# Low parts of eight weight units made by accumulating transfers instead of subtractions, in the last stages of a one-layer hybrid decoder

## The chip, the cores and the metric

The kernel runs on one core of one Trainium2 chip. The metric is the device time of one execution in microseconds (us); of several runs the median is given. The core has five engines with a queue each, worked off in order: TensorE (PE) multiplies, VectorE (DVE) and ScalarE (ACT) work elementwise, GpSimd (POOL) and SyncE (SP) here mostly issue transfers (DMAs), which run on 16 DMA engines.

## The reference, cut to what matters

One layer is computed for 512 prompt tokens and 64 sample tokens, 576 together. All arrays are fp32. The part around the change is the end of the layer:

```
h2 = rms_norm(x, g_ffn)
x = x + (silu(h2 @ w_ffn_gate) * (h2 @ w_ffn_up)) @ w_ffn_down      # 1024 -> 2816 -> 1024
h3 = rms_norm(x, g_ple)
gate = sigmoid(h3 @ w_ple_gate)                                      # 1024 -> 1024
emb = p @ w_ple_proj                                                 # 256 -> 1024
x = x + gate * emb
y = rms_norm(x, g_final)
```

Ahead of it stand the pooling and recurrent branches, a merge and an output projection.

## The kernel before, in words

All activations lie transposed: a tile has 128 features on the partitions and 576 tokens in the free dimension, in two halves of 288. `res[0]` to `res[7]` hold the residual x.

**Hi and lo.** A product in nearly full fp32 precision is made of three: weight and activation are each split into a high part (rounded to fp32r) and a low part (the rest), and `mm` (lines 141 to 160) accumulates hi*hi (line 153), hi*lo (line 155) and lo*hi (line 157) in PSUM, for both halves: 6 matmuls for each block of 128 input features. A weight "unit" is a tile of 128 x 1024 floats (512 KB). Each unit is loaded by SP into `raw` (line 70, two buffers) and split into `whi` and `wlo` (line 74, three buffers each).

There are two ways to split. `split_piece` (lines 76 to 79) copies `raw` to `whi` on ScalarE and subtracts `raw - whi` into `wlo` on VectorE. `split_dma` (lines 81 to 91) copies `raw` to `whi` on ScalarE, but rounds the negated copy `-raw` into `wlo`, also on ScalarE (line 87), and then POOL issues a DMA that reads the unit from HBM once more and adds it into `wlo` (line 88). With `hi_first` the copy to `whi` is line 86, ahead of the negation. `split` (lines 93 to 99) chooses by whether it was given a source `src`.

**Order of units.** `seq` (lines 102 to 113) lists the units in the order of their use. Its last part is `plain0` = 36 to 43 (gate and up units of the FFN), then from `dn0` = 44 on four down units (44 to 47, for the last four of 22 blocks of FFN features) and eight units of `w_ple_gate` (48 to 55). `next_unit` (lines 131 to 135) hands out unit i and calls `ahead` (lines 117 to 129), which issues loads up to unit i+4 and splits up to unit i+2. Line 126 says which units are split by DMA. The last two units take buffers of their own (line 125).

**The stages around the change.** The FFN runs in pairs of products by a fast matrix scheme (`pair`, lines 969 to 1029, and `drain`, lines 1049 to 1057), TensorE's order there being fixed by `in_order` (line 137) which holds up to line 1238. Then come:

- the down stage (lines 1154 to 1168): for each of eight output blocks m, 24 matmuls on the activations `ac` with half a down unit (12 first for m = 0 and for m = 1, then the other 12 of each); PSUM banks "c", "d" for even m and "a", "b" for odd m, two buffers each. Then VectorE adds the two halves to `res[m]` (line 1166), `scale_split` makes the high part `h3h` on ScalarE (line 241) and the low part `h3l` on VectorE (line 242), and `add_square` makes the square on ScalarE (lines 249, 252) and adds it to `ssum` on VectorE (line 253);
- ahead of it in the program, the embedding's inputs: two tiles of `p` are loaded, copied and split (lines 1141 to 1147, `pth`, `ptl`), and the two tiles of `w_ple_proj` are loaded into one buffer `wpe` and split (lines 1148 to 1151);
- the gate stage (lines 1217 to 1235): embedding product 0 (12 matmuls), gate products 0 and 1 (48 each), with the norm's `rms` in the middle of gate product 1, embedding product 1, and products 2 and 3; then blocks 4 to 7 in two parts by tokens (lines 1241 to 1283), and the final norm.

Within the limits that are written out (`in_order`, `issue_after`, `high_priority`), a scheduler puts each engine's instructions in order, by the program's order and by when it takes their inputs to be ready. Each queue then waits in that order.

Of the kernel before, what the change touches and what calls it, by code (L numbers as in the profile page):

```python
# [28 lines left out]
def trunk(ctx: ExitStack, tc: tile.TileContext, a, o):  # L29
# [13 lines left out]
    def pool(name, bufs=1, space=None, side=None):  # L43
        es[name] = ExitStack()
        kw = {} if space is None else {"space": space}
        if side:
            kw["side"] = side
        es_pool[name] = es[name].enter_context(tc.tile_pool(name=name, bufs=bufs, reuse_waits="tile", **kw))
        return es_pool[name]
# [18 lines left out]
    def raw_load(src, n=1024):  # L68
        raw = wp.tile([P, 1024], F32, name="raw", tag="raw", bufs=2)
        nc.sync.dma_start(out=raw[:, 0:n], in_=src)  # L70
        return raw

    def hi_lo(pl=wp, tag="", bufs=3):
        return [pl.tile([P, 1024], F32R, name="w" + n, tag="w" + n + tag, bufs=bufs) for n in ("hi", "lo")]

    def split_piece(raw, u, cs):
        hi, lo = u
        nc.scalar.copy(out=hi[:, cs], in_=raw[:, cs])  # L78
        tt(out=lo[:, cs], in0=raw[:, cs], in1=hi[:, cs].bitcast(F32), op=SUB)  # L79

    def split_dma(raw, u, src, hi_first=False):

        n = src.shape[-1]
        raw, hi, lo = (t[:, 0:n] for t in (raw, *u))
        if hi_first:
            nc.scalar.copy(out=hi, in_=raw)
        neg = act(lo, raw, AF.Copy, scale=-1.0)  # L87
        nc.gpsimd.dma_start(out=lo, in_=src, accum_op=ADD)  # L88
        if not hi_first:
            with tc.issue_after(neg.ins):  # L90
                nc.scalar.copy(out=hi, in_=raw)  # L91

    def split(raw, n=1024, src=None, **kw):
        u = hi_lo(**kw)
        if src is None:
            split_piece(raw, u, slice(0, n))
        else:
            split_dma(raw, u, src, True)
        return u
# [5 lines left out]
    up0 = len(seq)  # L105
    seq += [up[i] for i in range(KD)]
    out0 = len(seq)
    seq += [a["w_out"][m] for m in range(KD)]
    plain0 = len(seq)
    for m in range(NPL):  # L110
        seq += [a["w_ffn_gate"][m], a["w_ffn_up"][m]]
    dn0 = len(seq)
# [4 lines left out]
    def ahead(n_raw, n_split):  # L117
        while state["raw"] < min(n_raw, state["lim"]):
            i = state["raw"]
            raws[i] = raw_load(seq[i], seq[i].shape[-1])  # L120
            state["raw"] += 1
        while state["split"] < min(n_split, state["lim"]):
            i = state["split"]

            kw = dict(pl=es_pool["fp"], tag="z", bufs=2) if i >= len(seq) - 2 else {}
            if plain0 <= i < dn0 or i in (dn0 + 1, dn0 + 2) or up0 + 4 <= i < out0 and i % 2:
                kw["src"] = seq[i]
            splits[i] = split(raws.pop(i), seq[i].shape[-1], **kw)
            state["split"] += 1

    def next_unit():
        i = state["use"]
        state["use"] += 1
        ahead(i + 5, i + 3)
        return splits.pop(i)
# [57 lines left out]
    for k in range(5, KD):  # L193
        load_x(k)
    state["raw"] = state["split"] = state["use"] = 2
    ahead(3, 0)


# [95 lines left out]
    for k in range(KD):  # L294
# [7 lines left out]
        with tc.high_priority(offset=-0):  # L302
# [4 lines left out]
            else:  # L307
                sq = tmp.tile([P, T], F32, name="sq", tag="ta")
                act(sq, res[k], AF.Square)
                tt(out=ssum2, in0=ssum2, in1=sq, op=ADD)  # L310
    last_add = tt(out=ssum, in0=ssum, in1=ssum2, op=ADD)
    ahead(5, 3)
    u2 = next_unit()
    mm(zp[2], u2, hx, ks=range(0, 3))
# [45 lines left out]
    def tmpa():  # L360
        return tmp.tile([P, T], F32, name="ta", tag="ta")
# [699 lines left out]
    fp = pool("fp")  # L1061
# [76 lines left out]
    fp = pool("fp")  # L1138
    pe, wpe = [], []
    hx3 = [(fp.tile([P, T], F32R, name=f"h3h{k}"), fp.tile([P, T], F32R, name=f"h3l{k}")) for k in range(KD)]  # L1140
    for k in range(2):
        pn = tmpa()
# [5 lines left out]
    for e in range(2):  # L1148
        pn = fp.tile([P, 1024], F32, name="wpe", tag="wpe", bufs=1)
        nc.sync.dma_start(out=pn, in_=a["w_ple_proj"][e])  # L1150
        wpe.append(split(pn, pl=fp, tag="e", bufs=2))
    ssum = pers.tile([P, T], F32, name="ssum", tag="ssum")
    pzs = [two_banks() for _ in range(2)]
    u = next_unit()
# [193 lines left out]
def build(shapes):  # L1348
    import concourse.bacc as _bacc
    nc = _bacc.Bacc("TRN2", target_bir_lowering=False, num_devices=1, dynamic_dma_scratch_size=4096)  # L1350
    a = {n: nc.dram_tensor(f"in_{n}", s, F32, kind="ExternalInput").ap() for n, s in shapes.items()}
    o = {n: nc.dram_tensor(f"out_{n}", s, F32, kind="ExternalOutput").ap() for n, s in _OUTS}
    with tile.TileContext(nc, schedule_with_timeline_sim=False) as tc:
        trunk(tc, a, o)
    return nc
# [16 lines left out]
```

## Time and profile before

| | us |
|---|---|
| median of three runs | 836.67 (836.52 to 840.22) |
| the profiled execution, its time | 838.23 |
| its span, first to last instruction | 836.2 |
| TensorE busy | 822.1 (98%) |
| VectorE busy | 605.6 (72%) |
| ScalarE busy | 504.5 (60%) |
| GpSimd busy | 114.1 (14%) |

A row of the timeline gives the start in us from the span's start, the duration in us, the engine (PE, DVE, ACT, POOL, SP), the line of the kernel, the operation, the tiles as out<-in, and, in square brackets, the idle time of the engine before it and what ended it. A matmul's duration of 0.29 us overlaps the next one's. The names `bc`, `bd`, `ba`, `bb` are PSUM banks. "DMA to landing" is the time from a transfer's issue until its data has arrived, as lowest, median and highest.

### The profile page before, as it was taken

The numbers are of one execution on the slowest core, as the hardware profiler recorded it, in microseconds if no ns is written. First come the engines' busy times: TensorE is split into PE (matmuls) and PEld (weight loads), VectorE is DVE, ScalarE is ACT, GpSimd is POOL, SyncE is SP. The second block draws the span as 40 slices with busy tenths as digits, with TensorE's granted clock in tenths as the row PEclk, the third lists the DMA queues.
The fourth block names the chain that finished last, engine by engine and source line by source line (L and its number), as shares of the span: only waits on it lengthen the run. The fifth ranks groups of instructions, "written<-read, shape, count | busy, mean of one in ns | idle before, by whom it ended". The sixth has DMA issues, their size and how long they took to land.

```text
span 836.2 us, 15184 instructions
## 1 busy us (share of the span) xinstructions
PE 822.1 (98%) x6092; PEld 807.7 (97%) x6092; DVE 605.6 (72%) x1005; ACT 504.5 (60%) x826; POOL 114.1 (14%) x194
## 2 busy tenths in 40 slices
PE   8999999999999999999999999999999999999996
PEld 6999899999999999999999999999999999998996
DVE  7877776764787776547988688777787777558846
ACT  7356435666777665446667667766676666645534
POOL 6304110000111110000111121112211121000000
PEclk9999999999999999999999999999999999999998
DMA  7521220322747674246866787657777678453103
GB/s 233 164 84 51 76 105 29 126 105 80 181 107 183 165 172 140 76 108 144 186 130 142 149 208 194 157 123 175 181 173 164 132 158 214 113 156 101 52 1 113
DMA packets 38758, 111.95 MB, mean 134 GB/s; under 512 B 4896, under 2 KB 8992, under 8 KB 38688
## 3 DMA queue, kind: packets, MB, share of 16 engines
q1 hardware_dynamic: 24000, 74.51, 27.1%
q0 software_dynamic: 12528, 33.30, 23.5%
q10 hardware_dynamic: 2160, 3.19, 1.0%
q8 instruction: 47, 0.77, 0.4%
q14 instruction: 23, 0.19, 0.1%
HBM read 105.98 MB, written 5.00 MB: 133 GB/s over the span
## 4 chain that ended last, share of the span: by engine, by line
PE 91%; DVE 3%; DMA 2%; ACT 1%; issue 1%; POOL 1%; SPq 0%; DVEq 0%
PE bb L872 7%; PE bb L873 7%; PE bb L874 7%; PE mm L155 5%; PE mm L153 5%; PE mm L157 5%; PE ba L874 4%; PE ba L873 4%; PE ba L872 4%; PE bd L874 2%; PE bd L873 2%; PE bd L872 2%; PE bc L873 2%; PE bc L874 2%; PE bc L872 2%; PE ba L153 2%
## 5 line engine op out<-in xcount | busy, mean ns | idle before, releaser
L78 ACT CAST whi<-raw 128x1024 fp32r<-128x1024 f32 (+2 forms) x48 | 46.6, 972 | 70.6 <-PE mm L155 32.8
L153 PE MATMUL mm<-hh,whi 128*128 128x288 f32 x320 | 71.2, 304 | 1.1 <-DVE ta L358 0.9
L155 PE MATMUL mm<-hl,whi 128*128 128x288 f32 x320 | 70.8, 301 | 1.3 <-DVE hl L242 1.3
L157 PE MATMUL mm<-hh,wlo 128*128 128x288 f32 x320 | 69.5, 299 | 0.4 <-DVE wlo L79 0.4
L87 ACT ACTIVATE wlo<-raw 128x1024 fp32r<-128x1024 f32 (+1 forms) x49 | 49.2, 1004 | 26.3 <-PE ba L874 18.4
L79 DVE TENSOR_TENSOR wlo<-raw,whi 128x1024 fp32r<-128x1024 f32 (+2 forms) x48 | 56.7, 1184 | 10.4 <-ACT whi L78 9.8
L857 DVE TENSOR_TENSOR clo<-raw,chi 128x1024 fp32r<-128x1024 f32 (+1 forms) x38 | 43.3, 1140 | 27.8 <-ACT chi L853 27.7
L153 PEld LDWEIGHTS mm<-hh,whi 128*128 128x128 f32 x320 | 52.9, 193 | 4.0 <-ACT whi L78 1.6
L155 PEld LDWEIGHTS mm<-hl,whi 128*128 128x128 f32 x320 | 52.3, 191 | 2.5 <-DVE hl L242 1.9
L157 PEld LDWEIGHTS mm<-hh,wlo 128*128 128x128 f32 x320 | 52.3, 191 | 0.7 <-DVE wlo L79 0.6
L857 DVE TENSOR_TENSOR wlo<-rb,whi 128x1024 fp32r<-128x1024 f32 (+1 forms) x38 | 43.3, 1139 | 10.9 <-ACT whi L853 10.7
L853 ACT CAST chi<-raw 128x1024 fp32r<-128x1024 f32 (+1 forms) x38 | 36.9, 971 | 9.8 <-DVE raw L849 9.8
L853 ACT CAST whi<-rb 128x1024 fp32r<-128x1024 f32 (+1 forms) x38 | 37.3, 982 | 6.3 <-PE bb L873 2.8
L87 ACT ACTIVATE dl<-rb 128x512 fp32r<-128x512 f32 (+1 forms) x38 | 22.7, 598 | 30.0 <-PE bc L874 28.2
L1006 ACT ACTIVATE bc<-bb 128x288 f32<-128x288 f32 x38 | 15.0, 395 | 41.6 <-PE bb L874 41.6
L91 ACT CAST whi<-raw 128x1024 fp32r<-128x1024 f32 (+1 forms) x37 | 36.0, 972 | 0.0
L843 DVE TENSOR_TENSOR rb<-rb 128x512 f32<-128x512 f32 (+1 forms) x38 | 24.6, 647 | 8.0 <-ACT dh L91 8.0
L882 DVE TENSOR_TENSOR cz<-bc,p 128x288 f32<-128x288 f32 x38 | 17.3, 456 | 14.6 <-PE bc L874 14.3
L879 DVE TENSOR_TENSOR cz<-bb,p 128x288 f32<-128x288 f32 x38 | 17.3, 456 | 14.2 <-PE bb L874 9.1
L848 DVE TENSOR_TENSOR raw<-raw,rb 128x512 f32<-128x512 f32 (+1 forms) x38 | 24.6, 647 | 1.2 <-ACT whi L91 0.5
L88 POOL DMA_DIRECT2D wlo<-in_w_ffn_gate x13 | 11.1, 855 | 103.8 <-ACT wlo L87 103.8
L849 DVE TENSOR_TENSOR raw<-raw 128x512 f32<-128x512 f32 (+1 forms) x38 | 24.6, 647 | 0.8
(789 smaller groups left out, 3227.6 us busy)
## 6 DMA issues: line engine op xcount, KB each, us to landing
raw<-in_w_in SPq DMA_DIRECT2D x26, 512.0 KB, 3.4
raw<-in_w_ffn_gate SPq DMA_DIRECT2D x13, 512.0 KB, 4.1
raw<-in_w_ffn_up SPq DMA_DIRECT2D x13, 512.0 KB, 5.3
wlo<-in_w_ffn_gate POOLq DMA_DIRECT2D x13, 512.0 KB, 5.5
wlo<-in_w_ffn_up POOLq DMA_DIRECT2D x13, 512.0 KB, 6.3
rb<-in_w_ffn_gate SPq DMA_DIRECT2D x9, 512.0 KB, 4.6
rb<-in_w_ffn_up SPq DMA_DIRECT2D x9, 512.0 KB, 5.3
raw<-in_w_dn SPq DMA_DIRECT2D x12, 384.0 KB, 3.7
```

The lines of the kernel that those rows point to most:

```text
L78: nc.scalar.copy(out=hi[:, cs], in_=raw[:, cs])
L79: tt(out=lo[:, cs], in0=raw[:, cs], in1=hi[:, cs].bitcast(F32), op=SUB)
L87: neg = act(lo, raw, AF.Copy, scale=-1.0)
L91: nc.scalar.copy(out=hi, in_=raw)
L153: nc.tensor.matmul(out=out[h], lhsT=wh, rhs=xh[:, h * HT:(h + 1) * HT], start=first, stop=False)
L155: nc.tensor.matmul(out=out[h], lhsT=wh, rhs=xl[:, h * HT:(h + 1) * HT], start=False, stop=False)
L157: i = nc.tensor.matmul(out=out[h], lhsT=wl, rhs=xh[:, h * HT:(h + 1) * HT], start=False, stop=last)
L853: nc.scalar.copy(out=tiles[0][:, 0:2 * q["W"]], in_=q[raw][:, 0:2 * q["W"]])
L857: tt(out=lo, in0=q[raw][:, 0:2 * q["W"]], in1=hi.bitcast(F32), op=SUB)
L872: nc.tensor.matmul(out=out, lhsT=wh, rhs=xh, start=k == 0 and not seeded, stop=False, **kw)
L873: nc.tensor.matmul(out=out, lhsT=wh, rhs=xl, start=False, stop=False, **kw)
L874: i = nc.tensor.matmul(out=out, lhsT=wl, rhs=xh, start=False, stop=k == n - 1, **kw)
```

## The change

`split_dma` takes the place of `split_piece` for eight units: down units 44 and 47 (45 and 46 had it before), gate units 48 to 51, and the two tiles of the embedding's projection. Units 52 to 55 keep the subtraction.

```diff
@@ -123,7 +123,7 @@
             i = state["split"]
 
             kw = dict(pl=es_pool["fp"], tag="z", bufs=2) if i >= len(seq) - 2 else {}
-            if plain0 <= i < dn0 or i in (dn0 + 1, dn0 + 2) or up0 + 4 <= i < out0 and i % 2:
+            if plain0 <= i < dn0 or dn0 <= i < dn0 + 8 or up0 + 4 <= i < out0 and i % 2:
                 kw["src"] = seq[i]
             splits[i] = split(raws.pop(i), seq[i].shape[-1], **kw)
             state["split"] += 1
@@ -1148,7 +1148,7 @@
     for e in range(2):
         pn = fp.tile([P, 1024], F32, name="wpe", tag="wpe", bufs=1)
         nc.sync.dma_start(out=pn, in_=a["w_ple_proj"][e])
-        wpe.append(split(pn, pl=fp, tag="e", bufs=2))
+        wpe.append(split(pn, src=a["w_ple_proj"][e], pl=fp, tag="e", bufs=2))
     ssum = pers.tile([P, T], F32, name="ssum", tag="ssum")
     pzs = [two_banks() for _ in range(2)]
     u = next_unit()
```

## The prediction

> **What bounds the kernel now.** I read the page first, then the waits of TensorE from 700 us to the end, then the three engines in order of time around the places where TensorE waits.
>
> ```profile
> span 836.2 us, 15184 instructions
> ...
> PE 822.1 (98%) x6092; PEld 807.7 (97%) x6092; DVE 605.6 (72%) x1005; ACT 504.5 (60%) x826; POOL 114.1 (14%) x194
> ```
>
> TensorE is the bound. Work taken from VectorE (DVE) can only pay where TensorE waits for VectorE, in the stage that is changed. The first column of the next answer is who waited for whom, then the sum, the times and the longest.
>
> ```profile
> PE bc L153 <- DVE res L1166: 2.6, 2, 1.8
> ```
>
> From 700 us on TensorE waits for VectorE at two matmuls of line 153, 2.6 us together, and otherwise only at the last norm. TensorE in order of time:
>
> ```profile
> 721.71 0.30 PE L872 MATMUL bb<-fs0h,chi 128*128 128x288 f32 x1
> ...
> 731.26 0.29 PE L153 MATMUL bc<-ahh,whi 128*128 128x288 f32 x1
> ...
> 743.92 0.30 PE L157 MATMUL bb<-ahh,wlo 128*128 128x288 f32 x1
> 745.00 0.40 PE L153 MATMUL bc<-ahh,whi 128*128 128x288 f32 x1 [0.78 <-DVE res L1166]
> ...
> 752.25 0.29 PE L157 MATMUL bc<-ahh,wlo 128*128 128x288 f32 x1
> ...
> 759.58 0.30 PE L157 MATMUL bd<-pth,wlo 128*128 128x288 f32 x1
> 761.73 0.37 PE L153 MATMUL bc<-h3h,whi 128*128 128x288 f32 x1 [1.85 <-DVE res L1166]
> 762.00 0.40 PE L153 MATMUL bd<-h3h,whi 128*128 128x288 f32 x1
> ```
>
> From 752.25 to 759.58 lie 55 matmuls (20 left of m=6, 24 of m=7, 11 of the first embedding): 0.133 us each. The down stage starts at 731.26. At m=4 TensorE could go on at 744.05 and starts at 745.00, 0.95 lost. The embedding ends at 759.71; the first gate product starts at 761.73, 2.02 lost, and 0.14 more since the second bank follows after 0.27 and not 0.13. Both matmuls wait for a PSUM bank that VectorE must first add into `res` (line 1166). VectorE there:
>
> ```profile
> 743.82 0.76 DVE L1146 TENSOR_TENSOR ptl<-ta,pth 128x576 fp32r<-128x576 f32 x1 [0.68 <-ACT pth L1145]
> 744.49 0.45 DVE L1166 TENSOR_TENSOR res<-bc,res 128x288 f32<-128x288 f32 x1
> ...
> 750.35 0.46 DVE L1166 TENSOR_TENSOR res<-bc,res 128x288 f32<-128x288 f32 x1
> ...
> 757.20 1.22 DVE L79 TENSOR_TENSOR wlo<-raw,whi 128x1024 fp32r<-128x1024 f32 x1
> 758.33 0.82 DVE L242 SCALAR_TENSOR_TENSOR h3l<-res,C,h3h 128x576 fp32r<-128x576 f32 x1
> 759.06 0.76 DVE L253 TENSOR_TENSOR ssum<-ssum,sq 128x576 f32<-128x576 f32 x1
> 759.73 0.82 DVE L242 SCALAR_TENSOR_TENSOR h3l<-res,C,h3h 128x576 fp32r<-128x576 f32 x1
> 760.46 0.76 DVE L253 TENSOR_TENSOR ssum<-ssum,sq 128x576 f32<-128x576 f32 x1
> 761.12 0.46 DVE L1166 TENSOR_TENSOR res<-bc,res 128x288 f32<-128x288 f32 x1
> 761.49 0.45 DVE L1166 TENSOR_TENSOR res<-bd,res 128x288 f32<-128x288 f32 x1
> ```
>
> The evictions of m=0 (744.49) stand in VectorE's queue behind `ptl`, which waited for its input. From there VectorE has no gap; two pairs of m take 750.35 to 761.12, 5.4 us each, of which one split of line 79 is 1.13 (757.20 to 758.33). The evictions of m=6 thus come at 761.12, when TensorE has done everything else. Now ScalarE (ACT):
>
> ```profile
> 717.08 1.06 ACT L78 CAST whi<-raw 128x1024 fp32r<-128x1024 f32 x1 [0.64 <-ACT ta L954]
> 718.75 0.40 ACT L982 ACTIVATE bb<-ba 128x288 f32<-128x288 f32 x1 [0.62 <-PE ba L874]
> ...
> 740.83 1.05 ACT L78 CAST whi<-wpe 128x1024 fp32r<-128x1024 f32 x1 [7.84 <-DMA wpe<-in_w_ple_proj]
> 743.11 0.68 ACT L1145 CAST pth<-ta 128x576 fp32r<-128x576 f32 x1 [1.23 <-DMA ta<-in_p]
> 743.69 1.04 ACT L78 CAST whi<-raw 128x1024 fp32r<-128x1024 f32 x1
> ...
> 747.27 1.04 ACT L78 CAST whi<-wpe 128x1024 fp32r<-128x1024 f32 x1
> ...
> 748.79 1.03 ACT L78 CAST whi<-raw 128x1024 fp32r<-128x1024 f32 x1
> ```
>
> The copy at 717.08 is the first down unit, at 743.69 the fourth, at 748.79 the first gate unit. The first wait, m=4, comes from the load of `p`: `pth` starts when it lands. The change takes nothing off that path, so I leave the 0.95 us as they are.
>
> **The change, part by part.** Eight splits lose a subtraction of 1.22 us on VectorE and get a negated copy on ScalarE, a DMA issue on POOL and a transfer. The kernel does this elsewhere already, in the output stage:
>
> ```profile
> 366.17 1.05 ACT L86 CAST whi<-raw 128x1024 fp32r<-128x1024 f32 x1 [4.00 <-PE bb L155]
> 367.12 1.05 ACT L87 ACTIVATE wlo<-raw 128x1024 fp32r<-128x1024 f32 x1
> 368.08 0.76 ACT L241 ACTIVATE hh<-res,C 128x576 fp32r<-128x576 f32 x1
> 368.74 0.67 ACT L252 ACTIVATE sq<-res 128x576 f32<-128x576 f32 x1
> 368.47 0.84 POOL L88 DMA_DIRECT2D wlo<-in_w_ffn_gate  x1 [49.37 <-ACT wlo L87]
> ```
>
> Copy and negation stand back to back, ahead of `hh`; each step of 1024 takes ScalarE 0.95, `hh` 0.66, a square 0.58 (0.67, less the 0.09 by which neighbours overlap). POOL issues 0.30 after the negation's end. How long the transfer takes, first for the two down units that have it already, then for all of line 88:
>
> ```profile
> L88 POOL DMA_DIRECT2D wlo<-in_w_dn x2: 844/852/860, 727.3 to 730.5; - x2
> ...
> DMA to landing us min/median/max: 8.2/9.4/10.5
> ```
> ```profile
> DMA to landing us min/median/max: 3.6/5.4/10.5
> ```
>
> *First down unit.* Copy 717.08, negation to 719.09, POOL at 719.4; landing 10.5 later at the worst, 729.9, it is there before the stage's start at 731.26. ScalarE's seed copy behind it moves from 718.75 to 719.0; TensorE adds to that bank at 721.71. Cost nothing; beyond these covers each us late would be a us.
>
> The loads (SP) of that time, issue by issue:
>
> ```profile
> 730.19 0.33 SPq L70 DMA_DIRECT2D raw<-in_w_ple_gate  x1
> 730.57 0.52 SPq L1150 DMA_DIRECT2D wpe<-in_w_ple_proj  x1
> 733.32 0.33 SPq L1143 DMA_DIRECT2D ta<-in_p  x1
> ...
> 747.20 0.33 SPq L70 DMA_DIRECT2D raw<-in_w_ple_gate  x1
> ```
>
> *VectorE and ScalarE, 744 to 762.* Here the wait changes hands. ScalarE: the fourth unit's copy 743.69, its negation 744.64 to 745.69, `h3h` of m=0 at 745.6, its square 746.3, `h3h` of m=1 746.9, then the second embedding tile's copy and negation 747.5 to 749.4, the square of m=1 749.4 to 750.1. VectorE adds that square at 750.1 and, 0.67 later, evicts m=2 at 750.8: no earlier than the 750.35 of now, in spite of two subtractions less, and 0.1 before TensorE wants the bank (four matmuls before 752.25). Next pair: gate unit 0 on ScalarE 750.0 to 751.9, then `h3h`, square, `h3h`, square to 754.5; VectorE follows with 0.73 and 0.67 each from 752.7 on and evicts m=4 at 755.5. Next: gate unit 1 754.4 to 756.3, `h3h` of m=4 756.3 and so on, last square done 758.9; VectorE runs its own 1.47 + 1.46 + 1.34 and evicts m=6 at 759.9, against 761.12. Gain at the bank: 1.2 us, not the four subtractions' 4.5, since ScalarE takes over the pace.
>
> *The fourth unit's low part.* TensorE reads it first at 752.25. Negation ended 745.69, POOL at 746.0, so 6.2 us are covered; more stalls TensorE at m=6. No row shows this transfer. Its floor is 3.6, its ceiling 10.5 (756.5, a stall of 4.25). The two rows of 8.2 and 10.5 are nearest: they were issued 3.2 apart, and this one follows the embedding's (negation to 742.85, POOL 743.1) by 2.9; but three loads ran beside those (730.19, 730.57, 733.32), and here chiefly one does, the next gate unit's. I take 7.3, between the median 5.4 and their 9.4: landing 753.3, a stall of 1.05. The embedding then ends at 760.76 and the gate product starts there, its banks being free at about 760.5 (759.9 plus the 0.6 from 761.12 to 761.73). So 0.97 sooner, and most of the second bank's 0.14 with it. I take 1.1.
>
> The Trainium skill, in "DMA: Bandwidth & Descriptors", section "Anatomy of one DMA — SWDGE (gpsimd) path", fits such a transfer as 2.0 us plus bytes over 436 GB/s, an estimate of 3.2 us for 512 KB. By that the low part lands at 749.2, nothing stalls, and the sum is the bank's 1.2. The rows of 5.4 and 8.2 to 10.5 say otherwise, and I go by them.
>
> *The other low parts.* Embedding 0 lands by 753.6 at the worst, used near 758. Gate unit 0: negation to 752.0, POOL 752.3, landing 757.7 to 762.8, read near 761.3: no stall at the middle, 1.5 at the worst. Gate units 1 to 3 have ScalarE's time while their buffers are one product (6.4 us) and more ahead. *Moved issues:* SP's load behind the fourth unit is released by the negation at 745.7, not by a subtraction at 747.2; it has time either way, but runs beside the transfer that is short of it. POOL has no other work here. On ScalarE the `h3h` of m=7 is late by one negation; its reader is the last eighth of a 6.4 us product, which covers it.
>
> Sum: 1.1 us less. The profiled execution took 838.23 us, 2.03 of it outside the span; it becomes 837.1. The median of the three runs before is 836.67; I predict **835.6**.
>
> **The rivals.** *The transfer is late (0.24; slower).* The same mechanism beyond my price: landing 10.5 after issue stalls m=6 by 4.25, the gate product starts at 763.96, 2.2 later than now: 838.9. It decides from a landing of 8.3 (754.3) on, where the stall eats the whole 2.02. For it: the two nearest rows. Against it: fewer loads beside. The Trainium skill, "DMA: Bandwidth & Descriptors", section "SWDGE vs HWDGE vs iDMA", has each DMA engine take turns between the software and hardware queues; by it loads lengthen this transfer, as 8.2 and 10.5 beside the median 5.4 show.
>
> *ScalarE takes all of it (0.14).* If the two copies of embedding tile 1 or gate unit 1 stand one place further ahead than I put them, the squares, and the evictions of m=6 behind them, come a further 0.95 later: 760.85, a gain of 0.3: 836.4.
>
> *The whole backlog goes (0.14).* If evictions are not queued behind the squares, the bank is free when the embedding ends and the low part is in time: 2.16 less, 834.5; with the 0.95 at m=4 too, 833.6.
>
> *POOL's order (0.05).* If the second embedding tile's transfer is queued before the fourth unit's, POOL waits for its negation (749.4), the unit follows at 750.6 and lands 5.4 to 10.5 later: stalls of 3.75 to 8.85, net 1.7 to 6.8 slower: 838.4 to 843.5.
>
> **How the numbers follow.** My forecast has 0.43. The range takes the forecast, ScalarE's case, most of the whole gain and the late transfer up to its ceiling: 834.2 to 838.9. What a measurement here can tell from no change is about 0.5%, 4.2 us. All of TensorE's recoverable waiting is 3.1 us (0.95 + 2.16), so faster by that much has 0.02. Slower by that much needs POOL's order beyond half of its span; I give slower that rival's whole 0.05. Within: 0.93.
>
> **What would show it.** Right: line 79 has eight subtractions less and line 88 eight issues more; VectorE has gaps after 745 and waits for ScalarE's squares; the wait of 1.85 us at the first gate product shrinks; a new wait of TensorE at line 157 near 752, for the fourth unit's low part, of about 1 us. Wrong: no such wait (the transfer is quick), or one over 2 us (it is late and the kernel slower); evictions of m=6 before 757 (ScalarE is not the pace); a TensorE wait at line 157 in the gate products. A time past 834.2 or 838.9 would mean that some other wait was moved.

## The result, and the profile after

| | before, us | after, us |
|---|---|---|
| median | 837.25 (836.48 to 840.22) | 844.26 (841.58 to 847.09) |
| the profiled execution | 838.23 | 845.88 |

The ratio is 1.0077, with a 95% interval of 1.0059 to 1.0096. The kernel became slower by 0.8%, above the top of the predicted range of 838.9. Ratios, here and below, are of the fast executions alone; a single one of all, in e8, was slow (1614.45 us, where the others of e8 took 836 to 841), and the reason is not known. The page of after begins:

```profile
span 844.2 us, 15197 instructions
...
PE 824.4 (98%) x6092; PEld 810.8 (96%) x6092; DVE 597.1 (71%) x997; ACT 512.0 (61%) x834; POOL 121.3 (14%) x202
```

The work moved as announced: VectorE has eight instructions fewer and 8.5 us less, ScalarE eight more, POOL eight more. The span grew by 8.0 us. Whom TensorE waited for from 700 us on:

```profile
PE bc L157 <- DMA wlo<-in_w_dn: 8.2, 1, 8.2
PE mm L1291 <- DVE sq L1191: 0.5, 1, 0.5
```

The two waits for `res` (2.6 us) are gone. In their place stands one wait of 8.2 us for the low part of a down unit. TensorE in order of time at that wait:

```profile
752.03 0.30 PE L155 MATMUL bd<-ahl,whi 128*128 128x288 f32 x1
760.48 0.61 PE L157 MATMUL bc<-ahh,wlo 128*128 128x288 f32 x1 [8.15 <-DMA wlo<-in_w_dn]
760.89 0.44 PE L157 MATMUL bd<-ahh,wlo 128*128 128x288 f32 x1
```

This is m = 6, four matmuls into it: the first reading of the fourth unit's low part. The row behind the wait shows a second cost: the next matmul starts 0.41 us later, not 0.13, and lasts 0.44 and not 0.30. To see why the transfer is late, read ScalarE backwards from it:

```profile
741.75 1.05 ACT L86 CAST whi<-wpe 128x1024 fp32r<-128x1024 f32 x1 [7.58 <-DMA wpe<-in_w_ple_proj]
742.70 0.67 ACT L1145 CAST pth<-ta 128x576 fp32r<-128x576 f32 x1
743.27 1.06 ACT L87 ACTIVATE wlo<-wpe 128x1024 fp32r<-128x1024 f32 x1
744.23 0.76 ACT L241 ACTIVATE h3h<-res,C 128x576 fp32r<-128x576 f32 x1
744.90 0.67 ACT L249 ACTIVATE ssum<-res 128x576 f32<-128x576 f32 x1
745.47 0.77 ACT L241 ACTIVATE h3h<-res,C 128x576 fp32r<-128x576 f32 x1
746.14 0.67 ACT L252 ACTIVATE sq<-res 128x576 f32<-128x576 f32 x1
746.72 1.04 ACT L86 CAST whi<-raw 128x1024 fp32r<-128x1024 f32 x1
748.05 1.05 ACT L86 CAST whi<-wpe 128x1024 fp32r<-128x1024 f32 x1 [0.30 <-DMA wpe<-in_w_ple_proj]
749.01 1.05 ACT L87 ACTIVATE wlo<-wpe 128x1024 fp32r<-128x1024 f32 x1
749.97 1.04 ACT L87 ACTIVATE wlo<-raw 128x1024 fp32r<-128x1024 f32 x1
```

The first three rows are the first embedding tile with `pth` between its copy and its negation. The next four are the high parts and squares of m = 0 and 1. Only then comes the fourth unit's copy (746.72), and its negation (749.97) stands behind the whole pair of the second embedding tile. POOL follows in that order:

```profile
750.36 0.86 POOL L88 DMA_DIRECT2D wlo<-in_w_ple_proj  x1 [4.89 <-ACT wlo L87]
751.31 0.86 POOL L88 DMA_DIRECT2D wlo<-in_w_dn  x1
```

The chain that ended last says how long that transfer took:

```profile
751.31 9.13 DMA wlo<-in_w_dn
```

So it was issued at 751.31, 0.86 us before it was wanted (752.17), and landed 9.13 us later. The views by windows (after the engines' busy times come TensorE's granted clock, the DMA share and GB/s) show the second cost:

```profile
752.00:756.00 4.00, 0.33 (x3) 0.09 (x1) 3.33 (x6) 4.00 (x6) 0.19 (x2) 0.96 0.98 200
756.00:760.00 4.00, 0.00 (x0) 0.00 (x0) 2.22 (x4) 2.92 (x5) 0.85 (x1) 0.50 1.02 248
760.00:764.00 4.00, 3.52 (x14) 3.52 (x15) 1.49 (x2) 1.03 (x2) 0.84 (x1) 0.50 1.05 283
764.00:768.00 4.00, 4.00 (x25) 4.00 (x25) 1.71 (x4) 1.35 (x2) 0.00 (x0) 0.76 0.81 184
```

TensorE stands still in the second row, and its clock falls to 0.50 and stays there into the fourth: 0.32 + 4 + 4 + 1.92 = 10.2 us at half clock (twice the missing share, times 4 us). Before has 1.00 in all of these, as in this one:

```profile
756.00:760.00 4.00, 3.88 (x30) 3.63 (x28) 4.00 (x8) 2.60 (x4) 0.00 (x0) 1.00 0.12 25
```

The rest of m = 6 (20 matmuls from 760.48) takes 4.97 us against 20 x 0.133 = 2.66, so 2.3 more.

The sum, from the first down matmul to the start of gate product 1: 252 matmuls lie between, 33.6 us at 0.133. Before takes 731.26 to 768.36 = 37.1, so it loses 3.5. After takes 732.44 to 776.85 = 44.4 and loses 10.8: the gap of 8.45 less one step, 8.3, the clock's 2.3, and 0.2 more of half clock in m = 7. The difference is +7.3; the medians differ by 7.0. (The two spans differ by 8.0: in this execution of after TensorE also reaches the stage 1.2 us later, and it needs 0.5 less behind it.)

And why the wait at m = 4, which I had left in place, is gone. VectorE after:

```profile
737.30 0.46 DVE L1166 TENSOR_TENSOR res<-bc,res 128x288 f32<-128x288 f32 x1 [2.15 <-PE bc L157]
...
743.40 0.76 DVE L1146 TENSOR_TENSOR ptl<-ta,pth 128x576 fp32r<-128x576 f32 x1 [5.28 <-ACT pth L1145]
```

The evictions of m = 0 now stand ahead of `ptl` (737.30 against 743.40); before they stood behind it, at 744.49. The scheduler has put VectorE's queue in another order too. The load of `p` also landed sooner, 8.0 us after its issue and not 9.8, but nothing that m = 4 needs stands behind it any longer.

### The profile page after: what moved, and what is told of

It is laid out like the page before. It is cut to its first block, busy times and chain, and to the rows that moved or that the text cites. A ratio compares the mean times of both kernels' runs of the same rounds, so it can differ in the third digit from the quotient of the medians.

```text
span 844.2 us, 15197 instructions
## 1 busy us (share of the span) xinstructions
PE 824.4 (98%) x6092; PEld 810.8 (96%) x6092; DVE 597.1 (71%) x997; ACT 512.0 (61%) x834; POOL 121.3 (14%) x202
## 4 chain that ended last, share of the span: by engine, by line
PE 91%; DMA 3%; ACT 2%; issue 1%; DVE 1%; POOL 1%; SPq 0%; DVEq 0%; POOLq 0%
PE bb L873 7%; PE bb L872 7%; PE bb L874 7%; PE mm L155 5%; PE mm L153 5%; PE mm L157 5%; PE ba L874 4%; PE ba L873 4%; PE ba L872 4%; PE bd L873 2%; PE bd L874 2%; PE bd L872 2%; PE bc L874 2%; PE bc L873 2%; PE bc L872 2%; PE bc L157 2%
## 5 line engine op out<-in xcount | busy, mean ns | idle before, releaser
L78 ACT CAST whi<-raw 128x1024 fp32r<-128x1024 f32 (+2 forms) x42 | 40.4, 962 | 69.5 <-PE mm L155 32.9
L87 ACT ACTIVATE wlo<-raw 128x1024 fp32r<-128x1024 f32 (+1 forms) x55 | 55.5, 1009 | 25.7 <-PE ba L874 18.8
L79 DVE TENSOR_TENSOR wlo<-raw,whi 128x1024 fp32r<-128x1024 f32 (+2 forms) x42 | 49.4, 1178 | 9.3 <-ACT whi L78 8.6
L853 ACT CAST whi<-rb 128x1024 fp32r<-128x1024 f32 (+1 forms) x38 | 37.3, 982 | 6.3 <-PE bb L873 2.8
L91 ACT CAST whi<-raw 128x1024 fp32r<-128x1024 f32 (+1 forms) x37 | 35.9, 971 | 0.0
L86 ACT CAST whi<-raw 128x1024 fp32r<-128x1024 f32 x18 | 18.8, 1047 | 18.2 <-PE bb L155 8.2
```

The costliest lines, as they stand in the source:

```text
L853: nc.scalar.copy(out=tiles[0][:, 0:2 * q["W"]], in_=q[raw][:, 0:2 * q["W"]])
```

## Experiments

Two theories stand against each other. **Queue**: the transfer is late because of the places that ScalarE's new instructions took in its queue; each part of the change by itself is harmless. **Traffic**: eight transfers more of 512 KB, with the loads beside them, make each one slow. The DMA share near 1.0 in the windows above speaks for traffic, against 0.12 to 0.40 there before. All runs are compared with before on the same chip (its median there is 837.39 us for e1 to e4, 837.90 for e5 to e8); "stage" is the stretch summed above, where before has 37.1 us. TensorE reaches the stage at 728.85 (e5) to 732.82 (e4) in the span's time, so times of two runs are compared counting from the first down matmul (731.26 in before, 732.44 in after).

| run | what is different | median, us | ratio (95%) | stage | longest wait | at half clock |
|---|---|---|---|---|---|---|
| after | | 844.26 | 1.0077 (1.0059 to 1.0096) | 44.4 | 8.15 | 10.2 |
| e1 | unit 47 subtracted | 837.70 | 1.0008 (0.9989 to 1.0027) | 38.6 | 3.24 | 3.4 |
| e2 | both embedding tiles subtracted | 837.79 | 0.9997 (0.9981 to 1.0013) | 36.4 | 0.95 | 0 |
| e3 | embedding later in the program | 840.90 | 1.0040 (1.0024 to 1.0057) | 41.2 | 5.44 | 6.8 |
| e4 | second embedding tile subtracted | 843.82 | 1.0072 (1.0050 to 1.0094) | 41.8 | 6.50 | 6.8 |
| e5 | negation ahead of the copy | 837.40 | 0.9993 (0.9974 to 1.0012) | 35.9 | 0.89 | 0 |
| e6 | before, with unit 47 by transfer | 836.40 | 0.9995 (0.9977 to 1.0013) | 36.3 | 1.04 | 0 |
| e7 | before, with loads and splits apart | 837.19 | 0.9991 (0.9971 to 1.0011) | 37.3 | 1.81 | 3.4 |
| e8 | before, with the embedding by transfer | 838.36 | 1.0009 (0.9990 to 1.0029) | 36.3 | 2.33 | 0 |

**e1, the fourth unit by subtraction.** All else is as in after.

```diff
-            if plain0 <= i < dn0 or dn0 <= i < dn0 + 8 or up0 + 4 <= i < out0 and i % 2:
+            if plain0 <= i < dn0 or i in range(dn0, dn0 + 8) and i != dn0 + 3 or up0 + 4 <= i < out0 and i % 2:
```

> The fourth down unit alone gets its subtraction back; the other seven splits stay transfers. Queue theory (the 8.2 us wait comes from where this unit's negation and transfer stand in ScalarE's and POOL's queues): no wait at the fourth unit; from the first down matmul to the first gate product 27.2 us (204 matmuls of 0.133) plus at most 3 for the first gate unit's low part, against 30.5 before and 38.0 after; time 2 us (0 to 3.3) under the kernel before, about 835. Traffic theory (too many transfers at once, wherever they stand): the first gate units' low parts come late in turn, a wait of 5 us or more in the first gate product, time 840 or more.

The slowdown is gone: seven transfers cost nothing that can be measured. The 2 us under before that the queue theory gave didn't come either, since TensorE still waits once, elsewhere. The waits from 700 us on:

```profile
PE bc L153 <- DVE res L1166: 3.2, 1, 3.2
```

It is the first gate product again, waiting for the evictions of m = 6, longer than before's 1.85. VectorE has idle time there, and its waits between 740 and 768 us are

```profile
DVE ptl L1146 <- ACT pth L1145: 6.2, 1, 6.2
DVE h3l L242 <- ACT h3h L241: 6.0, 7, 1.1
```

In before it waited 0.5 us for `h3h`. ScalarE has become what VectorE follows, as the prediction had it; what it had not is that each m's evictions stand behind the previous m's `h3l` and `ssum`, so that they come one by one in ScalarE's pace. The evictions of m = 6 begin at

```profile
762.31 0.45 DVE L1166 TENSOR_TENSOR res<-bc,res 128x288 f32<-128x288 f32 x1
```

That is 30.0 us after the first down matmul, and 29.9 in before (761.12): the gain at the bank, 1.2 predicted, is not there. The wait is 1.4 longer since TensorE, without the wait at m = 4, arrives 1.3 sooner.

**e2, both embedding tiles by subtraction.** The six units keep their transfers.

```diff
-        wpe.append(split(pn, src=a["w_ple_proj"][e], pl=fp, tag="e", bufs=2))
+        wpe.append(split(pn, pl=fp, tag="e", bufs=2))
```

> Both tiles of the embedding's projection get their subtraction back; the six down and gate units stay transfers. Queue theory: ScalarE negates the fourth unit right behind its copy, ahead of the first h3h, as the prediction had it; issue about 2.3 us after pth, landing 6 to 8 later, a wait of 0 to 2.5 us at the fourth unit; the wait at m=4 (0.95) is back; time 835 to 838. Traffic theory: the transfer lands 9 us after its issue all the same, a wait of 3 us or more, 838 to 841.

Here ScalarE's queue has the order that the prediction assumed for the whole change:

```profile
743.68 1.04 ACT L86 CAST whi<-raw 128x1024 fp32r<-128x1024 f32 x1
744.62 1.05 ACT L87 ACTIVATE wlo<-raw 128x1024 fp32r<-128x1024 f32 x1
745.88 0.78 ACT L241 ACTIVATE h3h<-res,C 128x576 fp32r<-128x576 f32 x1 [0.21 <-DVE res L1166]
```

Negation at 744.62 against the predicted 744.64, though the stage starts 1.25 us later here: counted from the first down matmul it is 1.3 us sooner than predicted, with `p` landing 1.5 sooner than in before. The issue and the landing of that transfer, then TensorE's waits:

```profile
745.97 0.85 POOL L88 DMA_DIRECT2D wlo<-in_w_dn  x1 [13.26 <-ACT wlo L87]
```
```profile
DMA to landing us min/median/max: 7.5/7.5/7.5
```
```profile
PE bc L153 <- DVE res L1166: 1.0, 1, 1.0
PE bc L157 <- DMA wlo<-in_w_dn: 0.6, 1, 0.6
```

The transfer is issued 6.8 us ahead of its reader (6.2 predicted) and lands in 7.5 (7.3), and the wait is 0.6 (1.05). The price of the transfer was right, and given that order so was the forecast of a change too small to measure. The wait of 0.95 at m = 4, which I expected back, is not there; the 0.95 of the table is at the first gate product.

**e3, all eight transfers, the embedding's loads and splits moved in the program to m = 2.**

```diff
-    for e in range(2):
+    def wpe_tile(e):
...
             u = u if m % 2 else next_unit()
+            if m == 2:
+                wpe_tile(0)
+                wpe_tile(1)
```

> All eight transfers kept; only the place in the program of the embedding tiles' loads and splits is moved behind the fourth unit's split. Queue theory: the fourth unit's negation follows its copy directly, its transfer is issued about 2.3 us sooner and alone, landing 7 to 8 after issue: a wait of 4 to 5 us in place of 8.2, time about 840 (838.5 to 841.5). Traffic theory: same number of transfers, same wait of 8, 843 to 845.

Behind the first embedding tile the fourth unit now has its pair without the second tile between:

```profile
747.31 1.04 ACT L86 CAST whi<-raw 128x1024 fp32r<-128x1024 f32 x1
748.25 1.05 ACT L87 ACTIVATE wlo<-raw 128x1024 fp32r<-128x1024 f32 x1
```

POOL issues at 749.60, counted from the first down matmul 1.4 sooner than in after (2.3 expected), and the transfer lands in 7.8, 1.3 quicker; TensorE waits 5.44, 2.7 less. In spite of the move the first tile's negation (743.87) and the work of m = 0 and 1 still stand in front. What the second tile had put between is out of the way, and that was worth a third of the wait.

**e4, only the second embedding tile by subtraction.**

```diff
-        wpe.append(split(pn, src=a["w_ple_proj"][e], pl=fp, tag="e", bufs=2))
+        wpe.append(split(pn, src=None if e else a["w_ple_proj"][e], pl=fp, tag="e", bufs=2))
```

> The second embedding tile alone gets its subtraction back. Queue theory: one negation (0.95) and one POOL issue (0.95) less stand ahead of the fourth unit's transfer, which is issued about 1 us sooner and no longer directly behind another: landing 7 to 7.5 after issue, a wait of 5 to 6.5 us, time 840.5 to 842.5. Traffic theory: one transfer less of eight, wait 7 to 8, 842.5 to 844.

The wait is 6.50, at the upper end of what the queue theory gave. The copy of the second tile remains, and it waits for its load ahead of the negation that matters:

```profile
748.87 1.06 ACT L78 CAST whi<-wpe 128x1024 fp32r<-128x1024 f32 x1 [0.65 <-DMA wpe<-in_w_ple_proj]
749.83 1.06 ACT L87 ACTIVATE wlo<-raw 128x1024 fp32r<-128x1024 f32 x1
```

POOL issues at 751.17, counted from the first down matmul 0.5 sooner than in after (1 expected), but with no other POOL transfer just ahead, and it lands in 8.0 and not 9.1. One subtraction taken back saves 1.65 us of wait and no more. The time, 843.82 (four executions), lies above the queue theory's range and inside that of traffic. The stage is 4.7 above before, the median 6.4: in the profiled execution TensorE reaches the stage 1.6 us later than in before, with two stretches of half clock in the earlier stage and not one (told below), so most of the rest isn't in the stage.

**e5, all eight transfers, the negation first.** From the first down unit on, `split_dma` is called without `hi_first`: it negates, lets POOL issue, and copies afterwards.

```diff
-            split_dma(raw, u, src, True)
+            split_dma(raw, u, src, state["split"] < dn0)
```

> All eight transfers kept; in each of the ten units split by transfer here ScalarE negates first and copies to the high part afterwards. Queue theory: the fourth unit's transfer is issued about 3 us sooner (near 748 where the changed kernel has 751.3); landing 7.5 after issue gives a wait of about 3.4 us at the fourth unit, half of it or less (1.4) if the transfer is quicker (5.4) because the load that the split sets free now starts after it and not just ahead of it; time 836 to 839.5. Traffic theory: eight transfers as before, wait 7 to 8, 843 or more.

Here the traffic is whole and the order is not. ScalarE now negates the fourth unit at 741.17, and POOL and TensorE's waits show

```profile
742.52 0.86 POOL L88 DMA_DIRECT2D wlo<-in_w_dn  x1 [4.12 <-ACT wlo L87]
```
```profile
PE bc L153 <- DVE res L1166: 0.9, 1, 0.9
PE bc L157 <- DMA wlo<-in_w_ple_gate: 0.8, 1, 0.8
```

and the landing of that transfer is

```profile
DMA to landing us min/median/max: 5.2/5.2/5.2
```

The transfer took 5.2 us and was there before TensorE wanted it at 748.57; a wait of 1.4 to 3.4 was expected. It is issued 5.2 us sooner than in after, counted from the first down matmul, where I expected 3 (2.0 of it because the first embedding tile's load took 7.8 us and not 10.0), and it is 3.9 shorter. The DMA share in the windows that follow is as high as in after:

```profile
744.00:748.00 4.00, 4.00 (x32) 4.00 (x31) 0.52 (x1) 4.00 (x6) 0.86 (x1) 1.00 1.00 175
...
752.00:756.00 4.00, 4.00 (x32) 3.96 (x30) 3.08 (x6) 3.63 (x5) 0.84 (x1) 1.00 0.97 206
756.00:760.00 4.00, 2.29 (x15) 1.78 (x13) 3.15 (x7) 2.66 (x4) 0.06 (x1) 1.00 1.04 241
```

A full DMA queue does not by itself make TensorE wait: traffic falls as the one cause. The sooner start alone would not have ended the wait, though. It is issued 13.7 us after the first down matmul and wanted at 19.7; with the 9.1 us of after some 3 us of wait would be left (an estimate from these numbers). The small wait that is new, 0.8, is for the first gate unit. Against before the kernel cannot be told apart (0.9974 to 1.0012), although its stage is 1.2 us shorter.

**e6, only the fourth unit by transfer, on before.**

```diff
-            if plain0 <= i < dn0 or i in (dn0 + 1, dn0 + 2) or up0 + 4 <= i < out0 and i % 2:
+            if plain0 <= i < dn0 or dn0 + 1 <= i < dn0 + 4 or up0 + 4 <= i < out0 and i % 2:
```

> The kernel before with one transfer more, that of the fourth down unit. Queue theory: with the embedding tiles as before, ScalarE negates this unit right behind its copy, the transfer is issued about 2.3 us after pth begins and lands 7 to 8 later: a wait of 0.5 to 1.5 us at the fourth unit, the wait at m=4 stays; time 836.5 to 838, no change. Transfer theory (this transfer is the cost by itself, wherever it stands): a wait of 5 us or more, 841 or more.

Copy 741.87, negation 742.81, issue 744.31, and the waits are short:

```profile
PE bc L153 <- DVE res L1166: 1.0, 1, 1.0
PE bc L157 <- DMA wlo<-in_w_dn: 0.8, 1, 0.8
```

The unit whose transfer costs 8.15 us in after costs 0.8 when nothing else is changed; it landed in 7.6. The wait at m = 4, which I expected to stay, is not there: the 1.0 is at the first gate product.

**e7, the backlog's own cause, on before.** The prediction laid the first wait on the late load of `p`. Here `p` has buffers of its own, and the embedding's tiles, still subtracted, are moved to m = 2 with the edit of e3.

```diff
-        pn = tmpa()
+        pn = fp.tile([P, T], F32, name="pn", tag="pn", bufs=2)
```

> The kernel before, no transfer added: the two tiles of p get buffers of their own, so that their loads do not wait for the last FFN products, and the embedding's tiles are loaded and split behind the fourth unit in the program. Theory of the order (before, VectorE's backlog came from its queue standing behind two loads, not from its work): both waits for evictions go, 27.2 to 28 us from the first down matmul to the first gate product against 30.5, 3 us (2 to 3.5) less time. Theory of the work (VectorE's subtractions are too much for the stage): the wait at the first gate product stays above 1 us, gain under 1.2.

The wait at m = 4 is gone; the other stays at 1.8:

```profile
PE bc L153 <- DVE res L1170: 1.8, 1, 1.8
```

I expected the backlog to go and some 3 us with it; nothing measurable came. The load still lands late (`pth` at 740.00), and VectorE, without a gap from 740.71 on, frees the bank only 1.3 us sooner than in before, as much sooner as TensorE now arrives. The first gate product starts after 29.2 us and not 30.5; the stage of this execution is no shorter for it, because 3.4 us at half clock follow. Loads and splits in each other's way explain the first wait, not the second, which the theory of the work had right.

**e8, only the two embedding tiles by transfer, on before.**

```diff
-        wpe.append(split(pn, pl=fp, tag="e", bufs=2))
+        wpe.append(split(pn, src=a["w_ple_proj"][e], pl=fp, tag="e", bufs=2))
```

> The kernel before with the embedding's two tiles by transfer, all down and gate units as before. Queue theory: the negation of the first tile moves the fourth unit's copy behind the work of m=0 and m=1 on ScalarE, but its low part is a subtraction and needs no transfer: no wait at it; the evictions of m=0 stand ahead of ptl and the wait at m=4 goes; a wait of 0 to 3 us at the first gate product; time 835 to 838. If the two embedding transfers cost by themselves: 839 or more.

No wait for a transfer; the bank's wait is 2.33 and that of m = 4 gone:

```profile
PE bc L153 <- DVE res L1166: 2.3, 1, 2.3
```

With e6 this is the other half: either part alone is free on before, and taking either out of after ends the loss (e1, e2), so it takes both. A kernel with these two parts and nothing else wasn't run. The loss is the fourth unit's place in a queue that the embedding's tiles have filled.

## Why the prediction was wrong

*The bound, right.* TensorE was the bound, and its waits in before came from VectorE's backlog. That neither is left in after is not the gain that was forecast: the one at m = 4 went with the new order, and the one at the first gate product is covered by the stall. Without the stall, in e1, it is 3.2.

*The first down unit, right.* Free, with a landing of 7.2 us.

*"The change takes nothing off that path", wrong but small.* The path went through VectorE's order, not only through the load of `p`. In after the order changed, and the 0.95 us at m = 4 went with it. In e2 and e6, where the order is that of before, `p` landed 10.1 to 10.4 us after the first down matmul and not 11.9, and there no such wait is listed either.

*ScalarE's order: the step that failed.* The prediction has "its negation 744.64 to 745.69, `h3h` of m=0 at 745.6", and the embedding's "negation to 742.85". It took the back-to-back pairs of the output stage for a rule, and slid the first tile's negation into the idle time ahead of `pth`. In after `pth` comes first, the negation follows at 743.27, and the work of m = 0 and 1 passes the fourth unit; its negation starts at 749.97. Counted from the first down matmul that is 4.1 us later than predicted, and the reader, without the wait at m = 4, comes 1.3 sooner: POOL issues 0.86 us ahead of the reader and not 6.2. The stall is 8.3 us where 1.05 was forecast; of the 7.2 more, 5.4 are this lost head start and 1.8 the transfer's length. e2 and e6 have the predicted order and about the predicted cost; e3 and e4 have parts of the new one, and parts of the wait. One more instruction ahead of the unit did not add its own 0.95, it came with another order: after and all five runs in which the first embedding tile is a transfer (e1, e3, e4, e5, e8) have the work of m = 0 and 1 ahead of the unit; e2 and e6, where it is subtracted in its old place, have not.

*The rival "POOL's order".* It is close to what came: the second tile's transfer queued first, the unit behind it at 751.31 (750.6 in the rival), a stall of 8.3 within "stalls of 3.75 to 8.85". But it laid this on POOL's queue alone, where ScalarE's own order had changed and POOL only followed, so that the band held is in part luck. Its chance of 0.05 was far too small: nothing in the trace of before said that the embedding's second pair would not pass the unit, and the row of 747.27 (that tile's copy, 3.6 us after the unit's) was the only ground for it.

*The transfer's price, right where it stood alone.* 7.3 predicted; 7.5, 7.6, 7.8 and 8.0 in e2, e6, e3 and e4, where POOL issued no other transfer in the 4 us ahead of it; 9.1 in after, issued 0.95 behind another, and 5.2 in e5. The 3.6 and 5.4 that served as floor and median are of all 87 transfers of line 88, 50 of them of 192 to 384 KB; the 49 into `wlo`, 37 of them whole units, took 4.7, 5.6 and 10.5 (lowest, median, highest). The choice of 7.3 holds with these too. That loads beside it lengthen a transfer, as the prediction read from 8.2 and 10.5 beside 5.4, stays open: no run changes the loads alone. By the fit that I cited from the Trainium skill, "DMA: Bandwidth & Descriptors", section "Anatomy of one DMA — SWDGE (gpsimd) path", it would have been 3.2; the shortest of this stage in any run, in e5, took 5.0.

*ScalarE takes over the pace, right in kind.* VectorE waits 6 to 7 us for `h3h` in e1 and after. The gain of 1.2 us that it was to leave at the bank is none in e1 (0.1 later), 0.7 in e2 and 2.2 in e5, where all eight are transfers, each counted from the first down matmul; in after the stall hides it.

*The clock, not considered.* The rival's price ended at 843.5 because the wait was counted once. A wait of that length also halves the clock for what follows: 2.5 us in after by the sum above. With that, less the 3.5 that before loses, after's own stall gives 8.3 + 2.5 - 3.5 = 7.3.

That the unit stands behind m = 0 and 1 is read from the queues, and e1 to e6 show what follows from it. Why the scheduler put it there, and whether by the readiness of the inputs, was not tried and stays open.

## What to carry to other kernels

When an edit adds instructions to an engine whose order a scheduler makes, the trace of before does not give the new order; price the edit for the worst place that its last consumer could get, and treat back-to-back pairs seen in another stage as one case among several. A transfer that replaces a computation has a start as well as a length: here the length was within 0.7 us of the forecast in four runs, and the head start over the reader was 5.4 us short. Two edits that are each free can share one queue and one deadline, so measure them one by one and together.

## What the runs showed of the hardware

**A wait of TensorE can be paid twice.** The stretches of half clock in and behind the waits sum to 10.2 us (after), 6.8 (e3, e4) and 3.4 (e1, e7): one, two or three times 3.4. The Trainium skill, "TensorE: Matmul & The Clock Gate", section "Part 1: The HAM clock gate (the "warmup" mystery)", says that the clock is halved after an idle window of about 3.4 us and given back after a busy one, the windows running free. The steps of 3.4 agree. That it takes a whole idle window does not: in e3 the clock falls 2.9 us into the wait (0.14 missing of the window from 752 to 756, and the wait begins at 751.98), with TensorE busy right ahead of it. In e7 such a stretch follows a wait of 1.81 us, at the end of the embedding,

```profile
760.00:764.00 4.00, 3.49 (x15) 3.40 (x16) 3.88 (x8) 3.23 (x5) 0.00 (x0) 0.62 0.00 0
764.00:768.00 4.00, 4.00 (x31) 4.00 (x31) 2.27 (x3) 0.97 (x2) 0.00 (x0) 0.95 0.33 117
```

(0.38 and 0.05 missing, 3.4 us at half), while 1.85 us in before and 2.33 us in e8 cost none. Whether the wait brought it on in e7 is not shown, since such stretches also come without one:

**The same happens with TensorE busy.** Between 100 and 200 us, where the change is not, the clock falls for 3.4 us at a time without a wait that the profile shows; in before once, in after and e4 twice. The windows of before:

```profile
130.00:140.00 10.00, 10.00 (x68) 9.71 (x67) 5.88 (x12) 7.21 (x11) 0.00 (x0) 0.85 0.16 52
140.00:150.00 10.00, 10.00 (x78) 9.72 (x77) 7.96 (x18) 3.62 (x6) 1.20 (x1) 0.98 0.34 107
```

(0.15 and 0.02 missing of 10 us each, 3.4 us at half). In e5's profiled execution, the fastest of its ten at 833.95 us, there is none. The spread of 6 to 7 us between executions of one kernel goes with the mean clock: of the 35 executions of before on one chip, the three with a mean clock of 0.998 span 831.2 to 833.9 us, the ten with 0.990 to 0.992 span 836.3 to 838.5. Beside that spread a difference of 1 us in the stage doesn't show in the medians.

**Transfers of one size took from 5.0 to 10.5 us.** All are of 512 KB and of line 88, in this stage of the runs. In e5, with the negation first, the three issued at 737.55, 742.52 and 745.19 landed in 5.0 to 5.2 us, and the other seven of that stage in 6.3 to 8.9; in after, with the copy first, the ten took 6.9 to 9.1. With the copy first the negation also releases the next load, which SP issues 0.3 us ahead of the transfer (744.36 and 744.62, 751.04 and 751.31 in after); in e5 it follows 1.3 and 4.3 us behind (738.80 and 746.80). Whether that makes the three quick wasn't tried by itself, and the seven others speak against its being the whole reason.
